# Output-projection weights and the gains of the cross norm: loaded at other places, multiplied in at other places, and one norm handed from VectorE to ScalarE

## The chip, the cores and the metric

One core of one Trainium2 chip runs the whole program. The metric is the device time of one execution in microseconds (us). A core has a matmul engine (TensorE, PE in the rows; its weight loads are listed as PEld), VectorE (DVE), ScalarE (ACT), GpSimd (POOL) and SyncE (SP), which here only issues DMA transfers. Each engine works through its own list of instructions in order and waits on semaphores for the others.

## The reference, cut to what matters

One layer of a decoder on 1024 tokens of width 1024, in fp32: two mixers side by side (a gated short convolution and a sparse attention of 8 heads, 512 columns each), an output projection, cross attention to 256 memory tokens, and a SwiGLU block. The piece around the change is:

```python
def rmsnorm(x, g):
    y = xf * lax.rsqrt(jnp.mean(xf * xf, axis=-1, keepdims=True) + EPS)
    return (y * g.astype(jnp.float32)).astype(x.dtype)

mixed = jnp.concatenate([rmsnorm(y_conv, norm_conv_out), rmsnorm(y_att, norm_attn_out)], axis=-1)
h = h + rmsnorm(mixed @ w_out, norm_mix_post)

hn = rmsnorm(h, norm_x_pre)
mn = rmsnorm(mem, norm_mem)
qx = (hn @ w_q_x).reshape(b, s, X_HEADS, X_HEAD_DIM)
```

The gains `norm_x_pre` scale the columns of `hn`, which are the rows of `w_q_x`: the product is the same whether they are multiplied into the one or into the other.

## The kernel before, in words

Every matrix product is three matmuls: each operand is split into a rounded part `h` and a remainder `l`, and `mm3` (lines 58 to 62) adds h·h, h·l and l·h in PSUM. `split` (lines 64 to 76) makes `h` on ScalarE (line 66) and `l` on VectorE (line 75 or 76). A product of a 128x128 weight tile with 512 columns is one instruction of PE.

The program runs in stages: projections of the input, the attention by tiles of 128 tokens (its last product of values ends at about 661 us of the profile) with other products filled in between, then the stage of the change, the cross attention, and the SwiGLU block. The stage of the change goes as follows. Tiles are named by their stage and token tile: `mixed_t` holds tile t of the mixers' result.

The convolution half of the output projection, `mix_conv` (line 840), is worked during the attention, its products in `pwc`, and lands in `mixed_t`. The attention half needs rows 4 to 7 of `w_out` (`wor_k`, split into `woh_k` and `wol_k` by `wo_weights`, line 863) and the attention's output in transposed form: tiles 0 to 6 come back from DRAM in pairs (`or_0`, `or_2`, `or_4`, `or_6`, line 879), tile 7 straight from PSUM (`pot`, transposed on PE at line 554). `put_o` splits each into `A_h` and `A_l`. `mix_mm` then multiplies tile by tile into `pwa_t` (tiles 0 and 1 together, k outermost), and `mix_evac` (line 1008) adds it to `mixed_t` on VectorE.

`project` (line 955) and `Post` (line 908) carry each tile on: the squares of `mixed_t` are summed on ScalarE (`scr`, line 928), its post norm multiplied and added to the residual `res` (lines 934 and 935, VectorE), `res` spilled to DRAM, its squares summed again, and the next norm, that of the cross attention, written over `mixed_t` (line 942, VectorE, one pass over 128x1024 with the scale of the row and `g_next`, the gains broadcast to all partitions). `turn_in` transposes that on PE (`ptr`, line 950) and splits it into `A_h`, `A_l`. The products with `w_q_x` (`pqx`, `qx_mm`) follow: its column tiles `wq_h_d` are loaded and split by `col_weights` (line 896); the first two are wanted after tile 7 of `pwa`.

The order on each engine is decided by the framework's scheduler from a simulated timeline: instructions are written as above, the scheduler interleaves them, and `issue_after` holds some back behind a named instruction. Tiles with `bufs` rotate through that many buffers, and a load into a buffer waits for the last reader of its old content. Pools on the "right" side take memory from the other end.

## Time and profile before

| | |
|---|---|
| median of 3 runs | 1660.38 us (1659.99 to 1666.0) |
| profiled execution | 1662.39 us |
| its span, from first to last instruction | 1660.7 us |
| mean granted clock of PE | 0.98 |
| busy share of the span: PE, DVE, ACT, POOL | 95 %, 61 %, 46 %, 27 % |

The profile is of one execution. PE is busy 95 % of the span, so the time of the program is that of PE's work, at the clock it is granted, plus PE's waits; a change in what the other engines do shows only where PE waits for them. In a timeline a row gives the start in us from the span's start, the time taken, engine, line and operation (tile written <- tiles read), and in brackets how long the engine idled before it and which instruction released it. Rows of one kind that follow each other are merged (x2 means two).

### The profile page before, as it was taken

The numbers are of one execution on the slowest core, as the hardware profiler recorded it, in microseconds if no ns is written. First come the engines' busy times: TensorE is split into PE (matmuls) and PEld (weight loads), VectorE is DVE, ScalarE is ACT, GpSimd is POOL, SyncE is SP. The second block draws the span as 40 slices with busy tenths as digits, with TensorE's granted clock in tenths as the row PEclk, the third lists the DMA queues.
The fourth block names the chain that finished last, engine by engine and source line by source line (L and its number), as shares of the span: only waits on it lengthen the run. The fifth ranks groups of instructions, "written<-read, shape, count | busy, mean of one in ns | idle before, by whom it ended". The sixth has DMA issues, their size and how long they took to land. (4 is left out here: it accounts for less than half of the span.)

```text
span 1660.7 us, 22653 instructions
## 1 busy us (share of the span) xinstructions
PE 1578.8 (95%) x8095; PEld 1315.2 (79%) x8095; DVE 1008.9 (61%) x1781; ACT 762.0 (46%) x1554; POOL 456.3 (27%) x498
## 2 busy tenths in 40 slices
PE   8898999999999999889998988899999999999997
PEld 6786778887998888678796767688888888788886
DVE  5664456667656683771187597567444444587575
ACT  6433334456776674552285455333323232344453
POOL 0212345344554240000043003565344442000000
PEclk9999999999999999999999999999999999999999
DMA  8234111112620000633342144553333221873351
GB/s 296 66 118 149 39 57 46 51 48 87 203 100 17 20 8 19 228 141 109 109 138 90 52 167 169 163 201 112 110 119 114 103 96 70 321 275 97 100 166 69
DMA packets 78641, 192.59 MB, mean 116 GB/s; under 512 B 9024, under 2 KB 12224, under 8 KB 78528
## 3 DMA queue, kind: packets, MB, share of 16 engines
q1 hardware_dynamic: 73056, 179.08, 31.9%
q10 hardware_dynamic: 4320, 7.87, 1.3%
q0 software_dynamic: 1152, 4.19, 0.7%
q8 instruction: 64, 1.05, 0.3%
q14 instruction: 49, 0.40, 0.1%
HBM read 140.25 MB, written 50.86 MB: 115 GB/s over the span
## 5 line engine op out<-in xcount | busy, mean ns | idle before, releaser
L75 DVE TENSOR_TENSOR tl<-pt,th 128x512 fp32r<-128x512 f32 (+2 forms) x168 | 102.5, 620 | 54.8 <-ACT th L66 52.2
L61 PE MATMUL dp<-dl,ah 128*128 128x512 f32 x308 | 121.2, 394 | 2.2 <-DVE dl L75 2.2
L66 ACT ACTIVATE th<-pt 128x512 fp32r<-128x512 f32 (+2 forms) x168 | 89.2, 544 | 71.3 <-PE pv L653 37.2
L62 PE MATMUL dp<-dh,al 128*128 128x512 f32 x308 | 120.8, 393 | 0.0
L60 PE MATMUL dp<-dh,ah 128*128 128x512 f32 x308 | 118.6, 393 | 0.5 <-ACT dh L66 0.5
L626 POOL TENSOR_SCALAR pw<-pw,rs,gate 128x64 f32<-128x64 f32 (+5 forms) x128 | 76.1, 605 | 115.7 <-DVE rs L624 76.3
L66 ACT ACTIVATE ah<-over_l 128x512 fp32r<-128x512 f32 x77 | 48.5, 630 | 104.0 <-PE dp L61 103.9
L75 DVE TENSOR_TENSOR al<-over_l,ah 128x512 fp32r<-128x512 f32 x77 | 53.2, 690 | 54.3 <-ACT ah L66 53.2
L1103 POOL TENSOR_SCALAR xe<-xe,xsm 128x256 f32<-128x256 f32 x32 | 21.8, 696 | 208.3 <-DVE xsm L1101 202.8
L626 POOL TENSOR_SCALAR ps<-ps,rs,gate 128x128 f32<-128x128 f32 (+7 forms) x64 | 53.6, 840 | 86.1 <-DVE rs L624 43.6
L589 DVE TENSOR_REDUCE nm<-s 128x1 f32<-128x128 f32 (+7 forms) x64 | 47.9, 752 | 38.3 <-PE s L519 38.1
L61 PEld LDWEIGHTS dp<-dl,ah 128*128 128x128 f32 x308 | 58.6, 190 | 14.7 <-DVE dl L75 2.6
L60 PEld LDWEIGHTS dp<-dh,ah 128*128 128x128 f32 x308 | 58.3, 190 | 13.1 <-ACT dh L66 0.9
L62 PEld LDWEIGHTS dp<-dh,al 128*128 128x128 f32 x308 | 58.6, 190 | 12.3
L594 DVE TENSOR_REDUCE nm<-s 128x1 f32<-128x640 f32 (+4 forms) x64 | 41.7, 652 | 41.1 <-PE s L519 40.8
L1456 POOL TENSOR_TENSOR s<-wu 128x512 f32<-128x512 f32 x22 | 30.9, 1405 | 121.4 <-DMA wu<-in_w_gu_dram 20.1
L604 ACT ACTIVATE ps<-s,nm 128x128 f32<-128x128 f32 (+7 forms) x64 | 47.4, 742 | 28.6 <-DVE nm L589 28.6
L609 ACT ACTIVATE pw<-s,nm 128x640 f32<-128x640 f32 (+4 forms) x64 | 42.2, 659 | 31.7 <-DVE nm L595 24.7
L1468 DVE TENSOR_TENSOR u<-pc,u 128x512 f32<-128x512 f32 x22 | 15.2, 691 | 62.9 <-PE pc L62 62.3
L635 PE MATMUL pt<-ident,pw 128*128 128x128 f32 (+1 forms) x304 | 50.2, 273 | 1.6 <-DVE rs L623 1.6
L623 DVE TENSOR_SCALAR rs<-sm 128x1 f32<-128x1 f32 (+1 forms) x128 | 31.2, 246 | 30.4 <-ACT pw L615 20.1
L1482 DVE TENSOR_TENSOR a<-pd,u 128x512 f32<-128x512 f32 x22 | 15.2, 690 | 56.7 <-PE pd L62 56.7
(1495 smaller groups left out, 5275.0 us busy)
## 6 DMA issues: line engine op xcount, KB each, us to landing
over_l<-act_d SPq DMA_DIRECT2D x77, 256.0 KB, 2.7
wg<-in_w_gu_dram SPq DMA_DIRECT2D x22, 512.0 KB, 3.3
wu<-in_w_gu_dram SPq DMA_DIRECT2D x22, 512.0 KB, 3.9
act_d<-a SPq DMA_DIRECT2D x44, 256.0 KB, 2.1
act_d<-as_as SPq DMA_DIRECT2D x33, 256.0 KB, 2.8
h_d<-res SPq DMA_DIRECT2D x16, 512.0 KB, 2.6
res<-h_d SPq DMA_DIRECT2D x16, 512.0 KB, 4.2
over_h<-in_w_down_dram SPq DMA_DIRECT2D x28, 256.0 KB, 5.4
```

Source lines behind the costliest of these rows:

```text
L60: PE.matmul(ps, sh, mh, start=first, stop=False, **kw)
L61: PE.matmul(ps, sh, ml, start=False, stop=False, **kw)
L62: PE.matmul(ps, sl, mh, start=False, stop=last, **kw)
L66: ACT.activation(hi, src, AF.Copy, scale=1.0 if scale is None else scale)
L75: return (DVE if lo_eng == "dve" else POOL).tensor_tensor(lo, src, f32(hi), op=ALU.subtract)
L589: DVE.tensor_reduce(nm[:, r, 0:1], ps[:, :self.ns], axis=AX.X, op=ALU.max, negate=True)
L594: DVE.tensor_reduce(nm[:, r, 1:2], ps[:, self.w0:CM], axis=AX.X, op=ALU.max, negate=True)
L604: ACT.activation(e[:, :self.ns], ps[:, :self.ns], AF.Exp, bias=nm[:, r, 0:1], accum_out=sm[:, r, 0:1])
L609: ACT.activation(e[:, w0:CM], ps[:, w0:CM], AF.Exp, bias=nm[:, r, 1:2], accum_out=sm[:, r, 1:2])
L623: DVE.tensor_scalar(rs[:, r, s0:s1], sm[:, r, s0:s1], 1e-30, None, op0=ALU.max)
L626: POOL.tensor_scalar(e[:, c0:c1], e[:, c0:c1], rs[:, r, x:x + 1], gt[:, gi:gi + 1], op0=ALU.mult, op1=ALU.mult)
L635: PE.transpose(pt[:m, (2 * x + r) * P:(2 * x + r + 1) * P], self.P[b][r][:, c:c + m], ident)
```

## The change

- `g_x`, the gains `norm_x_pre` as 128x8 (partition p, column k holds gain 128k+p), is loaded by a DMA of its own, written in the middle of the program; it waits for nothing, and the scheduler puts it at the program's start, in SP's queue between the loads of `convw` and the fourth of `pr_kv`.
- Loads and splits of `w_out` rows 4 to 7: `wor_4`, `wor_5`, `wor_6` and `or_0` go into a new pool `wr`, issued during the attention; `woh_4` and `wol_4` are split there too. `wor_7` follows the use of `wor_5`'s buffer. The other three splits stay behind the attention.
- The broadcast row `g_next` and its 512 KB load are dropped. The norm of the cross attention in `Post.norm` becomes one ScalarE instruction per tile (8 in all), which multiplies by the row's scale alone.
- `col_weights` multiplies each of the eight `wq` tiles by `g_x` on GpSimd, in place, before its split; its raw tile has 2 buffers everywhere (the later use had 3).

```diff
--- before.py
+++ after.py
@@ -136,6 +136,7 @@
     SP.dma_start(gains, a["gains"])
     g_u, g_mem, g_c = gains[:, 0:NK], gains[:, NK:2 * NK], gains[:, 2 * NK:3 * NK]
 
+    g_x = const.tile([P, NK], F32, name="g_x")
     convw = const.tile([P, NC, 3], F32, name="convw")
 
     ap, close_ap = open_pool("ap")
@@ -848,6 +849,23 @@
 
     for t in range(NT - 5):
         mix_conv(t)
+    wr, close_wr = open_pool("wr", side="right")
+    wh, wl = {}, {}
+    wh[NC], wl[NC] = (wr.tile([P, D], F32R, name=f"wo{c}_{NC}") for c in "hl")
+    wor = {}
+
+    def wo_load(k):
+        wor[k] = wr.tile([P, D], F32, tag="woraw", name=f"wor_{k}", bufs=3)
+        SP.dma_start(wor[k], a["w_out"][k])
+
+    def wo_split(k):
+        split(wh[k], wl[k], wor.pop(k), scale=g_c[:, k:k + 1])
+
+    with nc.allow_non_contiguous_dma("one row of gains as columns"):
+        SP.dma_start(g_x, a["norm_x_pre"].rearrange("(k p) -> p k", p=P))
+    for k in range(NC, NK - 1):
+        wo_load(k)
+    wo_split(NC)
     with tc.issue_after(last_score.ins):
         for t in range(NT - 5, NT):
             mix_conv(t)
@@ -855,15 +873,9 @@
     close_keep()
 
     wo, close_wo = open_pool("wo")
-    wh, wl = {}, {}
-    for k in range(NC, NK):
+    for k in range(NC + 1, NK):
         wh[k] = wo.tile([P, D], F32R, name=f"woh_{k}")
         wl[k] = wo.tile([P, D], F32R, name=f"wol_{k}")
-
-    def wo_weights(k):
-        raw = wo.tile([P, D], F32, tag="woraw", name=f"wor_{k}", bufs=3)
-        SP.dma_start(raw, a["w_out"][k])
-        split(wh[k], wl[k], raw, scale=g_c[:, k:k + 1])
 
     def put_o(t, o):
         at = slice(NC, NK), slice(t * P, (t + 1) * P)
@@ -871,13 +883,16 @@
 
     put_o(NT - 1, tiles_[NT - 1].po)
     for t in range(NT - 1):
-        if t < NC:
-            wo_weights(NC + t)
+        if 0 < t < NC:
+            wo_split(NC + t)
         if t % 2 == 0:
-            raw = wo.tile([P, 2, CONV], F32, tag="woraw", name=f"or_{t}", bufs=3)
+            raw = (wr if t == 0 else wo).tile([P, 2, CONV], F32, tag="woraw" if t == 0 else "or", name=f"or_{t}",
+                                              bufs=3 if t == 0 else 2)
             n = min(2, NT - 1 - t)
             last_o = SP.dma_start(raw[:, :n, :], o_d[t:t + n].rearrange("t p c -> p t c"))
         put_o(t, raw[:, t % 2, :])
+        if t == 1:
+            wo_load(NK - 1)
     close_psum()
     psum, close_psum = open_pool("psum_dense", 1, space=PSUM)
     banks.clear()
@@ -894,10 +909,11 @@
         return hi, lo
 
     def col_weights(pool, name, src, bufs):
-        raw = pool.tile([P, NK, P], F32, tag="craw", name=f"{name}r", bufs=bufs)
+        raw = pool.tile([P, NK, P], F32, tag="craw", name=f"{name}r", bufs=2)
         hi = pool.tile([P, NK, P], F32R, tag="chi", name=f"{name}h", bufs=bufs)
         lo = pool.tile([P, NK, P], F32R, tag="clo", name=f"{name}l", bufs=bufs)
         SP.dma_start(raw, src)
+        POOL.tensor_tensor(raw, raw, g_x.rearrange("p (k o) -> p k o", o=1).to_broadcast([P, NK, P]), op=ALU.mult)
         split(hi, lo, raw)
         return hi, lo
 
@@ -939,7 +955,10 @@
             ss = self.ss
             self.square(self.res, 2)
             rms_scale(ss[:, 3:4], ss[:, 2:3], D)
-            DVE.scalar_tensor_tensor(self.m, self.res, ss[:, 3:4], self.g_next, op0=ALU.mult, op1=ALU.mult)
+            if self.g_next is None:
+                ACT.activation(self.m, self.res, AF.Copy, scale=ss[:, 3:4])
+            else:
+                DVE.scalar_tensor_tensor(self.m, self.res, ss[:, 3:4], self.g_next, op0=ALU.mult, op1=ALU.mult)
 
     def turn_in(s, t, m):
         tk = slice(t * P, (t + 1) * P)
@@ -987,10 +1006,8 @@
 
     wt, close_wt = open_pool("wt")
     g_post = wt.tile([P, D], F32, name="g_post1")
-    g_next = wt.tile([P, D], F32, name="g_next1")
     with tc.issue_after(last_o.ins):
         SP.dma_start(g_post, row_bcast(a["norm_mix_post"]))
-        SP.dma_start(g_next, row_bcast(a["norm_x_pre"]))
     wps = {}
 
     def mix_mm(ts_):
@@ -1026,11 +1043,12 @@
                 qx_weights(wt, 0, 2)
         qx_mm(0, 0, d)
 
-    project(1, mix_mm, mix_evac, lambda t: a["x"][t * P:(t + 1) * P, :], h1_d, wt, g_post, g_next, qx_early)
+    project(1, mix_mm, mix_evac, lambda t: a["x"][t * P:(t + 1) * P, :], h1_d, wt, g_post, None, qx_early)
     for d in range(2):
         qx_mm(0, 1, d)
     close_wt()
     close_wo()
+    close_wr()
     close_mp()
 
 
@@ -1397,7 +1415,7 @@
     def ox_between(n):
         if n == 0:
             for n_, name in enumerate(("norm_x_post", "norm_ffn_pre")):
-                g = og.tile([P, D + (144 if n_ == 0 else 0)], F32, name=f"g_{name}")[:, :D]
+                g = og.tile([P, D + (136 if n_ == 0 else 0)], F32, name=f"g_{name}")[:, :D]
                 SP.dma_start(g, row_bcast(a[name]))
                 gains2.append(g)
         else:
```

The order of the instructions is moved at three places. The first is ScalarE's list at the end of the attention (`osb` is the sum of squares of the attention's tile 7, `pwc_7_*` the last convolution products). Before:

```order
L548 ACTIVATE osb_7_5275,ss_a_88<-otok_7_5658 128x512
L83 ACT_TABLE_LOAD
L83 ACTIVATE r_a_86<-ss_a_88,eps_73 128x8
L847 ACTIVATE mixed_7_7043<-pwc_7_1_7254,r_c_85 128x512
L66 ACTIVATE A_h_96<-pot_7_5661 128x4x128
L66 ACTIVATE woh_4_7273<-wor_4_7283,gains_90 128x1024
L66 ACTIVATE A_h_96<-or_0_7287 128x4x128 x2
L66 ACTIVATE woh_5_7275<-wor_5_7291,gains_90 128x1024
L66 ACTIVATE woh_6_7277<-wor_6_7297,gains_90 128x1024
```

and now:

```order
L848 ACTIVATE mixed_7_7044<-pwc_7_0_7255,r_c_85 128x512
L66 ACTIVATE A_h_97<-or_0_7296 128x4x128 x2
L66 ACTIVATE A_h_97<-or_2_7308 128x4x128 x2
L549 ACTIVATE osb_7_5276,ss_a_88<-otok_7_5659 128x512
L66 ACTIVATE woh_7_7292<-wor_7_7304,gains_90 128x1024
L83 ACT_TABLE_LOAD
L83 ACTIVATE r_a_86<-ss_a_88,eps_73 128x8
L848 ACTIVATE mixed_7_7044<-pwc_7_1_7269,r_c_85 128x512
L66 ACTIVATE A_h_97<-or_4_7316 128x4x128 x2
L66 ACTIVATE A_h_97<-pot_7_5662 128x4x128
L66 ACTIVATE A_h_97<-or_6_7322 128x4x128
L66 ACTIVATE wq_0_0h_7710<-wq_0_0r_7709 128x1024
```

The weights' splits `woh_5` and `woh_6` stand ahead of these rows now; the splits of `or_0` to `or_4` and of `woh_7` have moved ahead of that of `pot_7`. On PE `pwa_0` and `pwa_1` alternated by twos before; now six of `pwa_0` come first, and the first of `pwa_1` waits for VectorE's `A_l` of `pot_7`, whose PSUM bank it takes.

The second is VectorE's list where the first two tiles of the projection leave PSUM. Before:

```order
L75 TENSOR_TENSOR A_l_97<-or_4_7311,A_h_96 128x4x128 x2
L75 TENSOR_TENSOR A_l_97<-or_6_7317,A_h_96 128x4x128
L1008 SCALAR_TENSOR_TENSOR mixed_0_7036<-pwa_0_7332,r_a_86,mixed_0_7036 128x1024
L1008 SCALAR_TENSOR_TENSOR mixed_1_7037<-pwa_1_7333,r_a_86,mixed_1_7037 128x1024
L84 RECIPROCAL ss1_0_7383<-ss1_0_7383 128x1
L934 SCALAR_TENSOR_TENSOR mixed_0_7036<-mixed_0_7036,ss1_0_7383,g_post1_7328 128x1024
```

and now:

```order
L75 TENSOR_TENSOR A_l_98<-pot_7_5662,A_h_97 128x4x128
L75 TENSOR_TENSOR A_l_98<-or_6_7322,A_h_97 128x4x128
L75 TENSOR_TENSOR wq_0_0l_7711<-wq_0_0r_7709,wq_0_0h_7710 128x1024
L1025 SCALAR_TENSOR_TENSOR mixed_0_7037<-pwa_0_7335,r_a_86,mixed_0_7037 128x1024
L1025 SCALAR_TENSOR_TENSOR mixed_1_7038<-pwa_1_7336,r_a_86,mixed_1_7038 128x1024
L75 TENSOR_TENSOR wq_0_1l_7718<-wq_0_1r_7716,wq_0_1h_7717 128x1024
L84 RECIPROCAL ss1_0_7386<-ss1_0_7386 128x1
```

The remainder of the first query weight, `wq_0_0l`, stood behind the evacuation of `pwa_2` and `res1_1`; now it stands ahead of that of `pwa_0`, and that of the second, `wq_0_1l`, behind `pwa_1`. On ScalarE both `wq` splits stand ahead of `scr1_0_0`, and wait for GpSimd's multiplication.

The third is the end of the projection, the last tiles' norms. VectorE before:

```order
L934 SCALAR_TENSOR_TENSOR mixed_7_7043<-mixed_7_7043,ss1_7_7761,g_post1_7328 128x1024
L935 TENSOR_TENSOR res1_7_7762<-res1_7_7762,mixed_7_7043 128x1024
L75 TENSOR_TENSOR A_l_97<-ptr1_5_0_7743,A_h_96 128x4x128
L75 TENSOR_TENSOR A_l_97<-ptr1_5_1_7750,A_h_96 128x4x128
L84 RECIPROCAL ss1_6_7669<-ss1_6_7669 128x1
L942 SCALAR_TENSOR_TENSOR mixed_6_7042<-res1_6_7670,ss1_6_7669,g_next1_7329 128x1024
L84 RECIPROCAL ss1_7_7761<-ss1_7_7761 128x1
L942 SCALAR_TENSOR_TENSOR mixed_7_7043<-res1_7_7762,ss1_7_7761,g_next1_7329 128x1024
```

and ScalarE now:

```order
L944 ACTIVATE scr1_7_0_7769,ss1_7_7766<-mixed_7_7044 128x1024
L959 ACTIVATE mixed_5_7042<-res1_5_7618,ss1_5_7617 128x1024
L83 ACTIVATE ss1_7_7766<-ss1_7_7766,eps_73 128x1
L944 ACTIVATE scr1_6_2_7773,ss1_6_7672<-res1_6_7673 128x1024
L83 ACTIVATE ss1_6_7672<-ss1_6_7672,eps_73 128x1
L959 ACTIVATE mixed_6_7043<-res1_6_7673,ss1_6_7672 128x1024
L66 ACTIVATE A_h_97<-ptr1_5_0_7748 128x4x128
L66 ACTIVATE A_h_97<-ptr1_5_1_7755 128x4x128
```

The norms of line 942 are gone from VectorE's list; ScalarE has them as `mixed_5`, `mixed_6`, each behind the squares it needs (in the changed kernel line 944 is the squares, 959 the norm). The first product of the next weights, `pqx_0_0_1`, still stands behind the transposes of tile 6 on PE.

## Rows read from the trace of the kernel before

**Rows 1.** Waits of PE, 640 to 830 us: line, releaser: total, times, longest.

```profile
PE ptr L950 <- DVE ss L84: 4.2, 1, 4.2
...
PE pwa L60 <- DVE mixed L1008: 2.6, 1, 2.6
PE pwa L60 <- ACT A_h L66: 2.4, 1, 2.4
...
PE pwa L61 <- DVE wol L76: 0.8, 2, 0.5
```

**Rows 2.** Stretches: length; busy PE, PEld, DVE, ACT, POOL; granted clock, DMA, GB/s.

```profile
687.00:690.00 3.00, 3.00 (x9) 2.35 (x8) 2.47 (x5) 1.90 (x6) 0.00 (x0) 0.50 1.02 418
717.00:735.00 18.00, 14.54 (x80) 12.13 (x78) 17.89 (x24) 12.08 (x26) 0.00 (x0) 0.99 0.35 137
736.00:741.00 5.00, 5.00 (x17) 4.23 (x16) 2.33 (x3) 1.19 (x2) 0.00 (x0) 0.50 0.75 270
```

**Rows 3.** Waits of PE from 0 to 50 us, same columns as group 1.

```profile
PE pe L298 <- ACT cmp L286: 3.7, 1, 3.7
```

**Rows 4.** DMA queue from 1.0 to 2.2 us: packets, MB, share of 16 engines.

```profile
q1 hardware_dynamic: 129, 0.01, 8.6%
```

**Rows 5.** DMA queue from 6 to 16 us, same columns.

```profile
q1 hardware_dynamic: 1385, 3.77, 99.4%
```

**Rows 6.** Timeline of ACT near 42 us: start, us, operation [idle before <- releaser].

```profile
41.92 1.06 ACT L199 ACTIVATE xt<-xt 128x1024 f32<-128x1024 f32 x1 [1.27 <-DMA xt<-in_x_dram]
```

**Rows 7.** Timeline of ACT from 655 to 700 us.

```profile
668.63 0.59 ACT L66 ACTIVATE A_h<-pot 128x512 fp32r<-128x512 f32 x1
669.10 1.15 ACT L66 ACTIVATE woh<-wor,gains 128x1024 fp32r<-128x1024 f32 x1
...
693.27 1.06 ACT L66 ACTIVATE wq_0h<-wq_0r 128x1024 fp32r<-128x1024 f32 x1 [1.59 <-DMA wq_0r<-in_w_q_x_dram]
```

**Rows 8.** Timeline of PE from 660 to 692 us.

```profile
667.84 0.60 PE L554 MATMUL pot<-ident,otok 128*128 128x128 f32 x4
...
683.09 0.40 PE L62 MATMUL pwa<-woh,A_l 128*128 128x512 f32 x1
686.08 0.50 PE L60 MATMUL pwa<-woh,A_h 128*128 128x512 f32 x1 [2.60 <-DVE mixed L1008]
...
687.34 0.63 PE L61 MATMUL pwa<-wol,A_h 128*128 128x512 f32 x1
687.77 0.63 PE L62 MATMUL pwa<-woh,A_l 128*128 128x512 f32 x1
```

**Rows 9.** Timeline of SP from 600 to 700 us.

```profile
679.37 0.42 SPq L992 DMA_DIRECT2D g_post<-in_norm_mix_post_dram  x1
```

**Rows 10.** Timeline of POOL near 392 us.

```profile
392.09 2.38 POOL L75 TENSOR_TENSOR fw_13l<-fw_13r,fw_13h 128x1024 fp32r<-128x1024 f32 x1
```

**Rows 11.** Timeline of DVE near 392 us.

```profile
392.16 3.39 DVE L760 SCALAR_TENSOR_TENSOR zc<-z,convw,zc 128x1023 f32<-128x1023 f32 x1 [0.34 <-POOL zc L758]
```

**Rows 12.** Timeline of DVE from 655 to 700 us.

```profile
669.25 0.69 DVE L75 TENSOR_TENSOR A_l<-pot,A_h 128x512 fp32r<-128x512 f32 x1 [0.95 <-ACT A_h L66]
670.28 1.28 DVE L76 SCALAR_TENSOR_TENSOR wol<-wor,gains,woh 128x1024 fp32r<-128x1024 f32 x1 [0.35 <-ACT woh L66]
...
684.75 2.47 DVE L1008 SCALAR_TENSOR_TENSOR mixed<-pwa,r_a,mixed 128x1024 f32<-128x1024 f32 x2
...
695.77 1.22 DVE L75 TENSOR_TENSOR wq_0l<-wq_0r,wq_0h 128x1024 fp32r<-128x1024 f32 x1
```

**Rows 13.** Line 942: count: shortest/median/longest ns, first and last start.

```profile
L942 DVE SCALAR_TENSOR_TENSOR mixed<-res,ss,g_next x8: 1266/1275/1285, 698.1 to 735.7; 128x1024 f32<-128x1024 f32 x8
```

**Rows 14.** Timeline of PE from 715 to 748 us.

```profile
735.70 1.94 PE L950 MATMUL ptr<-ident,mixed 128*128 128x128 f32 x8 [4.16 <-DVE ss L84]
737.29 0.78 PE L60 MATMUL pqx<-A_h,wq_1h 128*128 128x512 f32 x1
```

**Rows 15.** Timeline of ACT from 715 to 756 us.

```profile
747.95 1.06 ACT L66 ACTIVATE wq_0h<-wq_0r 128x1024 fp32r<-128x1024 f32 x1 [0.41 <-ACT qe L1041]
```

## The prediction

> **What bounds the kernel now.** I read the share of busy time first: PE is busy 95 % of its span, so what counts is where PE waits and at what clock it runs. The list of PE's waits around the projection shows what can be had there: 4.2 us for VectorE before the transposes of tile 6, 2.6 us for the evacuation of `pwa_0`, 2.4 us for the split of the attention's output, 0.8 us for weight remainders [rows 1], 10 us together. Behind the two gaps the table of stretches shows a granted clock of 0.50, the 1.2 GHz level, in 687 to 690 and in 736 to 741 us [rows 2]: products there started every 0.43 us [rows 8], and I count nine, against 0.25 in the stretch before (worked out below), so each such gap cost about 9 x 0.18 = 1.6 us more. At the program's start there is one more wait that the change can touch, 3.7 us for `cmp` [rows 3].
>
> **The change part by part.**
>
> *The load of `g_x`.* It is 1024 single values that lie 512 bytes apart in the tile's row order, so no two can share a run. The only small transfer whose packets stand alone is that of the gains, 128 rows of 96 bytes: 129 packets took 8.6 % of 16 engines over 1.2 us [rows 4], 1.65 us of one engine, 13 ns each. 1024 such packets are 13 us of one engine, 0.8 us of all 16. The other bound is the mean packet where `g_x` now goes: 1385 packets filled 99.4 % of the queue for 10 us [rows 5], 115 ns each, which makes 1024 x 115 / 16 = 7.4 us. The queue has no room there, so what `g_x` takes, the later loads come later: the last `xt` already keeps ScalarE waiting 1.27 us [rows 6], and behind its squares come `r_u`, `cmp` and PE's 3.7 us. I pass the delay on in full, and take the near row with a little for the full queue: +1.0 us, bounds 0 and +7.4.
>
> The Trainium skill has a rule that speaks against this load: "DMA: Bandwidth & Descriptors", section "Rules for kernel authors", says that a strided last dimension is lowered to one descriptor per element and should be rearranged. No row of before shows such a transfer. Were it gathered by rows, 128 packets, the term would be 0.1 us.
>
> *`woh_4` and `wol_4` in the attention.* One split is 1.15 us on ScalarE [rows 7] and 1.28 us on VectorE [rows 12]. Both have idle time there, PE has nearly none. I cost it +0.3 us; without cover it is 2.4 us, and the slight reshuffle of the attention may also give back 1 us.
>
> *The end of the attention.* The transposes of `pot` start at 667.84 us and take 0.60 [rows 8]. Before, `pwa_0` then waited 2.4 us. Now weight 4 and `or_0` are there, and six products of `pwa_0` run at once, to about 669.8. The next, the first of `pwa_1`, takes the bank of `pot` and waits for the remainder `A_l` of `pot_7`. In ScalarE's list that split (668.63 before) now has six splits `A_h<-or` of its own size and one `woh` ahead of it, 6 x 0.59 + 1.15 = 4.7 us [rows 7], of which I let 0.6 fit into its idle time (my estimate): it starts at about 672.7, and VectorE's part ends 1.3 us later, as before (669.25 + 0.69 - 668.63) [rows 7, 12], at 674.0. So the wait of 2.4 becomes one of about 4. Before, 48 products took from 670.8 (668.44 and the wait) to 683.5, with 0.8 us of waits in it: 0.247 each [rows 1, 8]. 42 of them from 674.0 end at 684.4, 0.9 us later than before; if this gap lowers the clock as the others did, 1.6 us later still.
>
> *Loads of the query weights.* Before, 13.9 us went by from the issue of `g_post` at 679.37 [rows 9] to the landing of `wq_0r`, which released ScalarE at 693.27 [rows 7]. Now `g_post` follows `or_6`, which waits for VectorE's split of `or_2` at about 668.3; and 512 KB of `g_next` are gone, about an eighth of what was in that queue, 1.3 us. With a less crowded queue I take the landing at 680.5 (679 to 682).
>
> *VectorE at the first evacuation.* `wq_0_0l` now stands ahead of it and waits for GpSimd, then ScalarE. GpSimd's product of two 128x1024 tiles takes 2.38 us [rows 10], ScalarE's part 1.06 [rows 7], the remainder 1.22 and an evacuation 1.24 (two in 2.47) [rows 12]. One more thing: beside that GpSimd product a VectorE instruction with two operands in SBUF took 3.39 us [rows 11], where one of the same form takes 1.28 [rows 13]; it ended about one such length after GpSimd did. The second multiplication (`wq_0_1`) follows the first at once, so `wq_0_0l` will be held until it ends: 680.5 + 2 x 2.38 + 1.22 + 1.24 = 687.7. Without that hold it is 680.5 + 2.38 + 1.06 + 1.22 + 1.24 = 686.4; by the products alone, 684.4 + 1.3 = 685.7, or 687.3 at the low clock. `pwa_2` started at 686.08 before [rows 8]. I take 687.8: +1.7 us (bounds -0.4 and +3.5). What waits behind `wq_0_0l` are both evacuations, so PE itself. The low clock behind this gap stays as it was.
>
> *The norms.* Eight instructions of 1.275 us [rows 13] leave VectorE, 10.2 us, and ScalarE gets eight of about 1.06 (its pass over a 128x1024 tile, as for `wq_0h` [rows 7]). In the middle of the projection PE does not wait for them. At the end it does: VectorE is busy 17.9 of the 18 us from 717 to 735 [rows 2], and its norm of tile 6 lets the transposes start at 735.70 after 4.16 us of waiting; they take 1.94 at the low clock, so that `pqx` goes on at 737.29 [rows 14]. Two norms stood on VectorE ahead of that of tile 6 in its last ten microseconds, and its own: without them tile 6's residual is done about 2.5 us earlier, and its norm, on ScalarE behind the squares, at about 731.2. PE is then still at the transposes of tile 5, which end at 731.5; those of tile 6 take about half of 1.94 at full clock, and `pqx` goes on at 732.5 to 733.0 instead of 737.29. With the gap goes the low clock behind it. That is -4.5 - 1.6 = -6.1 us (bounds -4.2 and -6.6). Next late would be tile 7's transposes: its norm by the same count at 736.3, before the 24 products of `pqx` end at 738.
>
> *The later query weights.* Six more multiplications, 2.38 each, and one raw buffer less. Their splits did not wait for loads before: the first, at 747.95, was released by ScalarE's own work [rows 15]. I take 0; if the chain of two buffers is late once, +2.4.
>
> Sum: 1.0 + 0.3 + 1.7 - 6.1 = -3.1 us, 1659.3 us for an execution like the profiled one (1662.39, of which 1660.7 are its span). That one lies 2.0 us over the median, so beside the runs shown the forecast is 1660.38 - 3.1 = 1657.3 us.
>
> **The rivals.**
>
> *The preload pays in full.* If the split of `pot_7` is early and the query weights land before the evacuations want them, the 48 products run from 668.45, end at 680.3, and `pwa_2` starts at 681.7, 4.4 us before its old time; a gap that short may leave the clock up, 1.6 more. With the norms, the start and the attention: -6.0 - 6.1 + 1.3 = -10.8, 1649.6 us. For it: the loads are early. Against it: the order of ScalarE's list.
>
> *Slower: the query weight holds VectorE.* Each us by which `wq_0_0r` lands after 680.5 moves the evacuation of `pwa_0`, and PE with it, by one. If SP's queue is not earlier than before and it lands at 693.3, that is +12.8 on the forecast, 1670.1 us. It turns the change into a loss once the landing is later than 680.5 + 3.1 = 683.6. For it: seven loads of 512 KB still share the queue there. Against it: SP's loads hang on instructions that come ten us earlier.
>
> *Slower: one packet per value at the price of the full queue.* 7.4 us in place of 1.0 makes 1663.7 us, 3.3 over before. For it: the queue is full, and the packets stand ahead of loads that PE wants. Against it: the mean packet carries 2.7 KB, `g_x`'s four bytes. The Trainium skill's rule named above is the one by which the packets are that many.
>
> *The norms do not help.* If ScalarE, which now has squares, splits and norms in one list, is as late with tile 6 as VectorE was, the term of -6.1 is gone: 1663.4 us. For it: the norm of tile 5 and that of tile 6 both stand behind squares there. Against it: ScalarE was idle for several us on either side of that place.
>
> **How the numbers follow.** Chances: forecast 0.55 (its own range 1653 to 1661), full preload 0.10, query weight late 0.13, packets dear 0.12, norms no help 0.10. A measurement of this kernel can tell about 0.5 % from no change, 8.3 us: under 1652.1 is faster, over 1668.7 slower. Under it lie the full preload and a rest of the forecast, 0.13; over it half of the late query weight and some mishap with the attention's order, 0.08; the rest, 0.79, is within. The range of 1650 to 1666 leaves out most of the full preload and of the late query weight, and takes in the other cases.
>
> **What would show it.** The transposes of tile 6 without a wait, and `pqx` behind them at full clock, show the norms' term; a wait for `ptr` or a granted clock of 0.50 there shows it wrong. The first product of `pwa_1` with about 4 us of waiting for VectorE's `A_l`, and `pwa_2` waiting for `mixed` until about 687.8, show the two junctions; `wq_0_0l` longer than 1.22 us shows the hold. The wait of `pe` for `cmp`, 3.7 before, shows the price of `g_x`. The forecast is wrong if PE's waits in 640 to 750 us do not shrink by some 3 us together, or if the time moves in stages that the change does not touch.

## The result: 0.6 % slower, and where the time went

The changed kernel takes 1673.02 us (median of 8 runs, 1667.55 to 1674.97) against 1662.87 of the kernel before on the same chip (8 runs, 1659.99 to 1666.0). The ratio is 1.0057, 95 % interval 1.0038 to 1.0075. The forecast was 1657.3 us, 3.1 less than the 1660.38 known then, and the range ended at 1666. The forecast is wrong in sign. The profiled execution took 1669.5 us with a span of 1667.8, 7.1 more than before, at the same mean clock (0.981 and 0.98). Line numbers have moved: 298 is now 299, 942 is 959 (on ScalarE) or 961, 950 is 969, 1008 is 1025; 865 loads `g_x`, 916 multiplies by it.

### The stage of the change: near the forecast, and faster

The waits of PE in the profile after, 640 to 760 us (line, releaser: total, times, longest):

```profile
PE pwa L60 <- DVE A_l L75: 3.6, 1, 3.6
PE pqx L60 <- DVE A_l L75: 1.0, 1, 1.0
PE pwa L60 <- DVE mixed L1025: 0.7, 1, 0.7
...
PE ptr L969 <- DVE A_l L75: 0.5, 1, 0.5
```

The 4.2 us before the transposes of tile 6 are gone, and the 2.6 for `pwa_0`'s evacuation are 0.7; in place of the 2.4 for `A_h` [rows 1] stand 3.6 for the `A_l` of `pot_7`. PE's timeline after (start, us, operation, idle before) shows the three places:

```profile
672.34 0.60 PE L555 MATMUL pot<-ident,otok 128*128 128x128 f32 x4
672.69 0.48 PE L60 MATMUL pwa<-woh,A_h 128*128 128x512 f32 x1
...
677.91 0.80 PE L60 MATMUL pwa<-woh,A_h 128*128 128x512 f32 x1 [3.58 <-DVE A_l L75]
678.51 0.63 PE L61 MATMUL pwa<-wol,A_h 128*128 128x512 f32 x1
...
691.24 0.50 PE L60 MATMUL pwa<-woh,A_h 128*128 128x512 f32 x1 [0.72 <-DVE mixed L1025]
...
736.42 0.66 PE L969 MATMUL ptr<-ident,mixed 128*128 128x128 f32 x4 [0.54 <-DVE A_l L75]
737.02 0.51 PE L60 MATMUL pqx<-A_h,wq_1h 128*128 128x512 f32 x1
```

The transposes of `pot` start 4.5 us later than before (667.84 [rows 8]), since what lies ahead took longer. Six products of `pwa_0` run at once, then comes the gap of 3.6 us, and behind it products start every 0.43 us instead of 0.23. At the end `pqx` follows the transposes without the old gap. The table of stretches of the same profile (columns as in [rows 2]):

```profile
679.00:683.00 4.00, 4.00 (x11) 3.13 (x10) 0.00 (x0) 0.00 (x0) 0.00 (x0) 0.50 1.03 420
717.00:735.00 18.00, 18.00 (x95) 15.04 (x94) 15.02 (x21) 15.01 (x28) 0.00 (x0) 1.00 0.35 133
736.00:741.00 5.00, 4.58 (x21) 3.69 (x22) 2.32 (x5) 3.47 (x7) 0.88 (x1) 1.00 0.84 277
```

The clock of 0.50 now lies behind the new gap, and no longer behind 736 us; from 717 to 735 PE has no idle time. The eight norms on ScalarE:

```profile
L959 ACT ACTIVATE mixed<-res,ss x8: 1138/1151/1159, 701.0 to 738.5; 128x1024 f32<-128x1024 f32 x8
```

They take 1.15 us each where the sum had 1.06, and end in time. The query weights, in the timelines of SP, POOL, ACT and DVE after:

```profile
675.91 0.53 SPq L915 DMA_DIRECT2D wq_0r<-in_w_q_x_dram  x1
```

```profile
685.15 1.90 POOL L916 TENSOR_TENSOR wq_0r<-wq_0r,g_x 128x1024 f32<-128x1024 f32 x1 [39.04 <-DMA wq_0r<-in_w_q_x_dram]
687.01 1.90 POOL L916 TENSOR_TENSOR wq_1r<-wq_1r,g_x 128x1024 f32<-128x1024 f32 x1
```

```profile
676.36 0.58 ACT L66 ACTIVATE A_h<-pot 128x512 fp32r<-128x512 f32 x1
...
687.08 1.06 ACT L66 ACTIVATE wq_0h<-wq_0r 128x1024 fp32r<-128x1024 f32 x1 [9.63 <-POOL wq_0r L916]
```

```profile
677.18 0.68 DVE L75 TENSOR_TENSOR A_l<-pot,A_h 128x512 fp32r<-128x512 f32 x1
...
688.17 1.81 DVE L75 TENSOR_TENSOR wq_0l<-wq_0r,wq_0h 128x1024 fp32r<-128x1024 f32 x1 [9.72 <-ACT wq_0h L66]
689.91 2.46 DVE L1025 SCALAR_TENSOR_TENSOR mixed<-pwa,r_a,mixed 128x1024 f32<-128x1024 f32 x2
```

`wq_0_0l` stands ahead of the evacuation, as the order showed, and takes 1.81 us instead of 1.22 [rows 12] beside the second multiplication. From the start of `pot`'s transposes to that of the last row of transposes of `mixed_7` PE took 77.0 us before and 70.4 now. Six more kernels further down have the instructions of before in this stage, and took 73.2 to 76.7 us there: the profile of before is the longest of the seven.

### The stage that no edit is in: slower

The table of stretches shows where the time went. From 1100 to 1400 us both kernels work the gate and up products of the SwiGLU block, from 1500 to 1640 its down products. Before, in the columns of [rows 2]:

```profile
1100.00:1400.00 300.00, 300.00 (x1312) 246.26 (x1311) 158.15 (x214) 93.14 (x145) 133.90 (x101) 1.00 0.33 111
1500.00:1640.00 140.00, 140.00 (x619) 115.98 (x618) 94.76 (x146) 65.96 (x117) 0.00 (x0) 1.00 0.35 106
```

and after:

```profile
1100.00:1400.00 300.00, 300.00 (x1287) 241.35 (x1286) 153.51 (x210) 91.55 (x142) 130.17 (x98) 1.00 0.32 109
1500.00:1640.00 140.00, 140.00 (x620) 115.91 (x619) 99.00 (x153) 67.77 (x121) 0.00 (x0) 1.00 0.36 110
```

PE never idles in either, the granted clock is 1.00 in both, and yet 1312 products have become 1287: one every 0.2331 us instead of every 0.2287. The down products are as fast as before (620 and 619). The whole gate and up stage took 381.98 us before and 389.39 now: 7.4 us, more than the 7.1 between the two spans, and three quarters of the 10.2 between the medians. The other stages of the two profiles nearly cancel: +1.3 us up to the first `pcv`, +3.2 in the attention, -6.6 in the projection, +1.3 in the query stage, +0.4 in the cross attention, +0.1 behind the gate and up products. In PE's own rows the products after, one behind the other, read

```profile
1199.67 0.40 PE L61 MATMUL pd<-xR_l,s_9h 128*128 128x512 f32 x1
1199.90 0.39 PE L62 MATMUL pd<-xR_h,s_9l 128*128 128x512 f32 x1
1200.14 0.39 PE L60 MATMUL pd<-xR_h,s_9h 128*128 128x512 f32 x1
1200.37 0.40 PE L61 MATMUL pd<-xR_l,s_9h 128*128 128x512 f32 x1
```

No row shows a wait: the pitch itself has changed.

What differs for these products is where their operands lie in SBUF. `g_x` is a tile of 32 bytes in each partition in the pool `const`, which is laid out first, so every later tile of the left side moves up by 32 bytes; the tiles of the right side stay. The gate and up products have the moving operand (`x_*`, `xR_*`) on the left and the stationary one (the split weights, `s_*` and the like) on the right; the down products have both on the right. By the sizes of the tiles the moving operands start at 288 bytes, modulo 1024, before and at 320 after, the stationary ones at 992: their distance was 704 and is 672. This is the distance of the tiles' starts. The blocks of a weight tile lie 512 bytes apart (128 values), so the products of every second block have 512 less, 192 before and 160 now. The down products' operands both start at 864: distance 0. The diff itself answers to the shift at one place: the padding in `ox_between` goes from 144 to 136 values, 32 bytes less, which keeps the tiles behind it where they were.

### The profile page after: what moved, and what is told of

It reads as the page before. It is cut to its first block, busy times and chain, and to the rows that moved or that the text cites. A ratio compares the mean times of both kernels' runs of the same rounds, so it can differ in the third digit from the quotient of the medians.

```text
span 1667.8 us, 22673 instructions
## 1 busy us (share of the span) xinstructions
PE 1588.2 (95%) x8095; PEld 1313.0 (79%) x8095; DVE 998.4 (60%) x1773; ACT 770.4 (46%) x1562; POOL 471.0 (28%) x506
## 3 DMA queue, kind: packets, MB, share of 16 engines
q8 instruction: 64, 1.05, 0.3%
## 5 line engine op out<-in xcount | busy, mean ns | idle before, releaser
L1486 DVE TENSOR_TENSOR u<-pc,u 128x512 f32<-128x512 f32 x22 | 15.2, 692 | 64.8 <-PE pc L62 64.2
L636 PE MATMUL pt<-ident,ps 128*128 128x128 f32 x288 | 48.5, 283 | 1.3 <-DVE tl L75 1.3
```

The costliest lines, as they stand in the source:

```text
L636: PE.transpose(pt[:m, (2 * x + r) * P:(2 * x + r + 1) * P], self.P[b][r][:, c:c + m], ident)
```

## The experiments

All kernels ran in five rounds beside the kernel before. "Distance" is that of the stationary from the moving operand of the gate and up products, modulo 1024 bytes. The stages are worked out from the starts of rows in PE's timelines, as the profile merges them: attention from the first `pcv` to the last `pot`, projection from there to the last `ptr` of the stage, query stage on to the first `psx`, gate and up from the first `pd` to the first `dp`; each from one profile. The ratio is to the kernel before, with its 95 % interval.

| kernel | distance | attention | projection | query | gate, up | ratio |
|---|---|---|---|---|---|---|
| before | 704 | 505.3 | 77.0 | 82.55 | 381.98 | |
| after | 672 | 508.5 | 70.4 | 83.82 | 389.39 | 1.0057 (1.0038 to 1.0075) |
| e1: before, left +32 | 672 | 514.1 | 76.0 | 83.82 | 389.39 | 1.0095 (1.0069 to 1.0120) |
| e2: before, left +64 | 640 | 508.6 | 74.2 | 83.86 | 387.79 | 1.0069 (1.0043 to 1.0096) |
| e3: before, left +32, right -32 | 640 | 510.1 | 73.2 | 83.85 | 387.79 | 1.0085 (1.0063 to 1.0106) |
| e4: after, left +32 more | 640 | 511.2 | 70.0 | 83.54 | 387.80 | 1.0069 (1.0047 to 1.0091) |
| e5: before, both -32 | 704 | 506.3 | 73.8 | 82.55 | 381.98 | 1.0004 (0.9988 to 1.0021) |
| e14: before, left -32 | 736 | 509.2 | 76.7 | 83.83 | 389.38 | 1.0071 (1.0044 to 1.0098) |
| e11: before, left -320 | 0 | 506.3 | 74.2 | 81.90 | 378.31 | 0.9971 (0.9953 to 0.9989) |
| e6: after, left at its old place | 704 | 505.6 | 71.9 | 82.55 | 381.98 | 1.0007 (0.9986 to 1.0028) |
| e9: norms and query weights alone | 704 | 506.4 | 70.9 | 82.58 | 382.00 | 0.9971 (0.9949 to 0.9993) |
| e10: output weights alone | 704 | 505.4 | 74.2 | 82.55 | 382.00 | 0.9991 (0.9970 to 1.0011) |
| e13: after's parts, reordered | 704 | 510.9 | 69.3 | 82.58 | 381.98 | 1.0003 (0.9984 to 1.0022) |
| e15: e13 better ordered, left -320 | 0 | 509.3 | 64.2 | 81.92 | 378.29 | 0.9922 (0.9894 to 0.9950) |

### Is it the address, and which one? e1 to e4

e1 and e2 are the kernel before, with 32 or 64 unused bytes behind `convw` and the padding cut by as much; e3 moves the left side by 32 and lays 32 unused bytes under the right side, too (with one memset of them on GpSimd); e4 is the changed kernel with `g_x` in 64 bytes.

```diff
-    convw = const.tile([P, NC, 3], F32, name="convw")
+    convw = const.tile([P, NC * 3 + 8], F32, name="convw")[:, :NC * 3].rearrange("p (c j) -> p c j", j=3)   # e1, e3; +16 in e2
...
+    rp, close_rp = open_pool("rp", side="right")                  # e3
+    rpad = rp.tile([P, 8], F32, name="rpad")
...
-    g_x = const.tile([P, NK], F32, name="g_x")                    # e4, from after
+    g_x = const.tile([P, 2 * NK], F32, name="g_x")[:, :NK]
```

> The kernel before, with nothing changed but 32 unused bytes per partition behind convw: every tile allocated from the left after it lies 32 bytes further, those from the right stay; the instructions and their order are those of before. Theory A (the products whose stationary and moving operands no longer lie at the same offset modulo 64 bytes run slower: conv products 300 to 380 us and the gate/up products 1053 to 1435 us, at 0.2333 us against 0.2285 per product): 7 to 7.5 us longer in 1053 to 1435 us, 1.5 us in 100 to 380, in all +8 to +10 us, about 1671. Rival B (the slower products of the changed kernel come from its instructions, or from the chip that ran it): no difference, 1660 to 1666.

> As e1, with 64 unused bytes instead of 32. Theory A (offset modulo 64): no difference from before, 1660 to 1666, and the gate/up products at 0.2285 us. Rival C (any move away from the old addresses, or less free memory, costs it): about +9, 1671.

> The kernel before with 32 bytes on the left and 32 on the right, so that both operands of all products move from offset 32 to offset 0 modulo 64. Theory A1 (it is the difference of the two operands' offsets that costs): no difference from before, 1660 to 1666. Theory A2 (it is the offset of the moving operand by itself): +9 or more, 1671 and above, and the down products (dp), whose operands both lie on the right, slower too.

> The changed kernel with the tile of g_x 64 bytes wide instead of 32 (only half is used): instructions and order as in the changed kernel, left tiles at offset 32 modulo 64 again. Theory A: the gate/up products at 0.2285 us again, 8 to 9 us less than the changed kernel, 1663 to 1665, so about -0.5 to +2 us against before; the forecast's own sum (-3.1) would be 1659.8 beside a median of 1662.9. Rival B (its instructions or the chip): 1673 as before the edit.

e1 has every instruction of before in its old order, and 32 unused bytes. It is slower by 0.95 % (0.69 to 1.20), 16 us (11 to 20), which more than covers the change's loss. Its gate and up products, and those of e3:

```profile
1100.00:1400.00 300.00, 300.00 (x1287) 241.34 (x1286) 154.71 (x210) 91.69 (x142) 132.10 (x100) 1.00 0.33 111
```

```profile
1100.00:1400.00 300.00, 300.00 (x1293) 243.19 (x1292) 157.32 (x213) 91.30 (x142) 132.53 (x100) 1.00 0.32 111
```

e1 counts 1287 products as the changed kernel does. That 64 bytes would restore the old speed, since only the address modulo 64 mattered, fell with e2 and e4. e3 has e1's left addresses and yet e2's 387.79 us, to the hundredth: the left address alone does not decide, the distance does.

### Equal distance at other addresses, and the parts at the old ones: e5, e6, e9, e10

e5 and e6 put two small tiles into one, which moves the left side down by 32 bytes; e5, from before, adds e3's right-side pool, e6, from after, the padding of 144. e9 has the norm on ScalarE and the multiplied query weights, with `g_x` as a fourth group in the load of `gains`, and nothing of the output weights; e10 has the output weights' part of the diff alone.

```diff
-    r_m = const.tile([P, 2], F32, name="r_m")                     # e5, e6, e9
-    ss_m = const.tile([P, 2], F32, name="ss_m")
+    rs_m = const.tile([P, 4], F32, name="rs_m")
+    r_m, ss_m = rs_m[:, 0:2], rs_m[:, 2:4]
...
-    gains = const.tile([P, 3 * NK], F32, name="gains")            # e9
+    gains = const.tile([P, 4 * NK], F32, name="gains")
+    g_x = gains[:, 3 * NK:4 * NK]
```

> The kernel before with two small tiles laid into one, which moves all later left tiles 32 bytes down, and 32 bytes taken at the top of the right side, which moves all right tiles 32 bytes down: the distance from every left tile to every right one is that of before, all absolute addresses differ. So far the gate/up stage (first pd to first dp) took 381.98 us before, 389.39 at a distance changed by 32 bytes (changed kernel, e1) and 387.79 at one changed by 64 (e2, e3, e4). Theory A1 (the distance between the two operands decides): 382.0 us there and no difference from before in all. Rival C (the old addresses by themselves are good): 387 to 390 and +8 to +12 in all.

> The changed kernel with the same two small tiles laid into one, so that g_x takes no new room: every tile that both kernels have and that the change does not move on purpose lies where it lay before, instructions and order as in the changed kernel. Theory A (the addresses are what the forecast missed): gate/up 382.0 us, 9 to 10 us less than the changed kernel in all, and so 0 to 4 us less than before (the forecast's sum was -3.1). Rival D (the changed kernel is slower for other reasons too, its clock in the attention or the junction): +3 or more against before.

> The kernel before with the norm part alone: g_x as eight more columns of the gains tile (no load of single values), multiplied into wq by GpSimd, the norm by ScalarE, g_next dropped; W_out's loads as before; addresses as before. Forecast's own terms: the tail's -6.1 and a junction of 0 to +1.7: -4 to -6 us against before, the 4.2 us of waiting before the transposes of tile 6 gone. Rival (the norms do not help, or the query weight in front of the evacuation eats it): -1 to +3.

> The kernel before with the W_out part alone (loads of rows 4 to 6 and of or_0, and the first split, during the attention), addresses of the other tiles as before. By the forecast: the 2.4 us wait of pwa_0 becomes one of 3.5 to 4 of pwa_1 for the split of pot_7, the low clock behind it costs 1.6: 0 to +2 us against before. Rival (the preload pays): -3 to -6, no wait above 1 us ahead of pwa.

e5 moved both sides, and nothing changed: 381.98 us, ratio 1.0004. Distance again, not address. e6 is the whole change without the shift: the gate and up stage is back at 381.98 and 1312 products, and the total at that of before (-2.3 to +4.7 us).

```profile
1100.00:1400.00 300.00, 300.00 (x1312) 246.15 (x1311) 158.99 (x214) 92.32 (x143) 132.90 (x101) 1.00 0.32 112
```

The waits from 640 to 760 us of e9, and then of e10:

```profile
PE pwa L60 <- ACT A_h L66: 2.4, 1, 2.4
PE pwa L60 <- DVE mixed L1011: 1.9, 1, 1.9
PE ptr L955 <- ACT mixed L945: 1.0, 2, 0.5
```

```profile
PE ptr L962 <- DVE ss L84: 4.2, 1, 4.2
PE pwa L60 <- DVE A_l L75: 3.5, 1, 3.5
```

The parts are separate: the norms cut the wait for `ptr` from 4.2 us to two of 0.5, and gain 0.29 % (0.07 to 0.51), 4.8 us; the output weights trade a wait of 2.4 for one of 3.5, and their total is unchanged within the interval.

### Another distance, and a better order: e11, e13, e14, e15

e14 is e5 without the right-side pool. e11 is the kernel before with `identb` and `ones` in a later pool of the left side (`keep`) and the merge of e5, so that `A_h` and the gate and up operands come 320 bytes lower. e13 holds the late splits behind `pot_7` and the `wq` multiplication behind the second evacuation, with `g_x` in `gains` as in e9, at the old distance; e15 writes `pot_7`'s split out so that ScalarE's part comes first, and adds distance 0 (for which `r_u` moves to `keep`, too).

```diff
-    identb = const.tile([P, P], BF, name="identb")                # e11, e15
+    identb = keep.tile([P, P], BF, name="identb")
...
-        put_o(t, raw[:, t % 2, :])                                # e13; hi7 in e15
+        with tc.issue_after(low7.ins) if t > 1 else ExitStack():
+            if t == NC - 1:
+                wo_split(NC + t)
+            put_o(t, raw[:, t % 2, :])
...
+        with tc.issue_after(behind) if behind is not None else ExitStack():   # behind = the evacuation of pwa_1
```

> The kernel before with the two small tiles laid into one: left tiles 32 bytes lower, right ones in place, a distance of 736 modulo 1024. By distance the gate/up stage took 381.98 us at 704, 389.39 at 672 and 387.79 at 640. Theory A1: not the value of before again, since the distance differs: 387 to 390, +8 to +12. Rival (only less distance costs, or only a move upwards): 382, no difference.

> The kernel before with two small const tiles laid into one and two others (identb, ones) allocated in the attention's pool, so that the tiles from A_h on and the gate/up operands lie 320 bytes lower: left operands (offset 288 modulo 1024 before) now at 992, like the right ones; instructions and order unchanged. The down products, whose operands lie at equal offsets modulo 1024 in every kernel, start every 0.2267 us on average, the gate/up products every 0.2285 before and 0.2325 to 0.2335 at the other distances. Theory E (equal offsets are the best distance): gate/up about 379 us instead of 381.98, conv products shorter too, -3 to -5 us in all. Rival F (the old distance of 704 was a lucky one, this one is like the rest): 387 to 390 and +8 to +12.

> The changed kernel at the old addresses, with g_x as columns of the gains tile, the splits of or_2 to or_6 and of woh_7 held behind that of pot_7, and GpSimd's multiplication and the splits of the first two query weights held behind the evacuation of tile 1. By the forecast's own steps the 3.5 us wait of pwa_1 and the low clock behind it go, and VectorE evacuates pwa_0 at once: the stretch from the last pot to the last ptr, 71.9 us with the changed kernel at old addresses (e6), 77.0 before, comes to 64 to 67; -7 to -10 us against before. Rival (another wait takes the place of these, the query weights come late for pqx): 70 and more there, -2 to 0.

> All parts together: the changed kernel with g_x as columns of the gains tile, ScalarE's split of pot_7 now held ahead of those of or_2 to or_6 and of woh_7 (in e13 only VectorE's part was held, and pwa_1 still waited 3.3 us), the query weights behind the evacuation of tile 1, and identb, ones and r_u allocated in the attention's pool, so that left and right operands lie at equal offsets modulo 1024 as in e11. By the terms measured so far: gate/up 378.3 us (-3.7), conv and query products about -1, the stretch from the last pot to the last ptr 64 to 67 us against 74 to 77 with the kernel before (e13 had 69.3 with the wait of 3.3): -9 to -13 us against before, ratio 0.992 to 0.995. Rival (the gains do not add, something next is late): -3 to -6 as e9 or e11 alone.

e14 is slower by 0.71 % though it saves 32 bytes: at 32 bytes either way from 704 the stage is as slow. The gate and up products of e14, and of e11, at distance 0:

```profile
1100.00:1400.00 300.00, 300.00 (x1288) 240.98 (x1287) 154.49 (x211) 90.34 (x140) 131.88 (x99) 1.00 0.33 111
```

```profile
1100.00:1400.00 300.00, 300.00 (x1325) 248.43 (x1324) 161.09 (x216) 92.88 (x144) 133.73 (x101) 1.00 0.34 114
```

e11 has 1325 products in the same 300 us, 0.2264 us each, which is the pitch of the down products (140 us through 619: 0.2262), whose distance is 0 in every kernel. e11 is 0.29 % (0.11 to 0.47) faster than before with none of its work changed.

e13 failed in its aim: only VectorE's part of `pot_7`'s split was held in front, and the wait stayed. The waits of e13, and of e15, from 640 to 760 us:

```profile
PE pwa L60 <- DVE A_l L75: 3.3, 1, 3.3
PE pwa L60 <- DVE mixed L1027: 1.5, 1, 1.5
PE ptr L971 <- ACT mixed L961: 1.3, 1, 1.3
```

```profile
PE pqx L60 <- DVE A_l L75: 1.0, 1, 1.0
...
PE pwa L60 <- DVE A_l L885: 0.5, 1, 0.5
```

e15 has both gaps closed, 64.2 us in the projection against 77.0, and the short pitch. It takes 1650.24 us, 0.78 % (0.50 to 1.06) less than before, 13 us: the fastest kernel here.

## Why the prediction was wrong

**The step that failed** is the sum, 1.0 + 0.3 + 1.7 - 6.1: it has a term for what each edit issues and none for where its tile lies. `g_x` was costed as a DMA alone; that its 32 bytes move every left-side operand against the right side was not weighed, though the diff shows the tile at the head of `const` and a padding that answers to it. The prediction named time that moves in stages the change does not touch only as a condition for being wrong. That condition came true: the term left out is +7.4 us in the gate and up stage and +1.3 in the query stage, 8.7 together, and e6, the change without the shift, is 0.5 % or 8 us better than the change. That is two thirds of the 12.6 us between the forecast of -3.1 and the +9.5 of the ratio; the rest, some 4 us, is what e6 misses, and is located below in one profile only.

The attention is longer, too, in the six kernels at 640, 672 and 736 (508.5 to 514.1 us, against 505.3 to 506.4 in the five at 704 in the order of before or of the change). But there it is the clock. The stretch from 395 to 450 us, before, after, in e1 and in e13:

```profile
395.00:450.00 55.00, 51.72 (x389) 47.28 (x390) 44.28 (x89) 41.81 (x86) 31.88 (x27) 0.97 0.58 191
395.00:450.00 55.00, 52.18 (x372) 47.24 (x371) 42.19 (x79) 38.54 (x82) 28.70 (x24) 0.91 0.54 178
395.00:450.00 55.00, 52.17 (x347) 47.27 (x346) 40.79 (x79) 38.55 (x79) 27.43 (x23) 0.84 0.54 178
395.00:450.00 55.00, 52.33 (x349) 47.46 (x348) 40.94 (x80) 38.91 (x80) 28.48 (x25) 0.84 0.53 178
```

By the clock records of the traces the attention had a granted clock of 0.50, half of the full one, for 5.5 us before, 11.4 after and 23.1 in e1. Half of what was added, 3.0 and 8.8 us, is what the stage is longer, 3.2 and 8.8. With half of that time taken off, the attention is 502.5 to 504.2 us in the six and 502.6 to 503.8 in the five. Whether the shift brings the low clock is open: e13 has it, too, at the old distance but in another order, with 510.9 us. By itself the shift costs 16 us (11 to 20) by e1, and 11 to 14 by e2, e3 and e14; 8.7 of e1's 16 are the two stages' pitch, and the rest is not located beyond its one profile.

**The norms, -6.1.** The mechanism was right: transposes without the wait, `pqx` at full clock, as written. The size is less sure. From the start of `pwa_2` to that `pqx` PE took 51.2 us before (686.08 to 737.29 [rows 8, 14]) and 45.8 after, -5.4 where the sum had -4.5. e9's total is 4.8 us shorter (1.2 to 8.5). That its projection is 6.1 shorter, the forecast to the tenth, is luck: against the other six profiles with the instructions of before, 73.2 to 76.7 us, it is 2.3 to 5.8.

**The end of the attention, +1.7 in all.** The mechanism was right and its sizes nearly so: a gap of 3.6 us for `pot_7`'s `A_l` where I said about 4, and the low clock behind it. Counted from the start of `pot`'s transposes, since all of it lies 4.5 us later, the query weight landed after 12.8 us (forecast 12.7), and `pwa_2` started after 18.9 (forecast 20.0). `wq_0_0l` was held as said: it ended at 689.98, 1.07 us after the second multiplication. But GpSimd's multiplications take 1.90 us instead of the 2.38 taken from a subtraction of two whole tiles (line 75, which the prediction calls a product). Taken together, the projection became 6.6 us shorter than in the profile of before, and 2.8 to 6.3 shorter than in the other six, where the sum had 1.7 - 6.1 = -4.4.

**The load of `g_x`, +1.0.** Its price in the queue is the near row's; its price in PE's time is not resolved. In the DMA part of the profile after (whole run, then the load from 0 to 40 us), and in ACT's timeline:

```profile
DMA packets 79537, 192.07 MB, mean 115 GB/s; under 512 B 10048, under 2 KB 13248, under 8 KB 79424
...
g_x<-in_norm_x_pre_dram SPq DMA_DIRECT2D x1, 4.0 KB, 6.8
```

```profile
42.97 1.06 ACT L200 ACTIVATE xt<-xt 128x1024 f32<-128x1024 f32 x1 [1.26 <-DMA xt<-in_x_dram]
```

Packets under 512 bytes were 9024 before: 1024 more, one for each value. This agrees with the rule of the Trainium skill, "DMA: Bandwidth & Descriptors", section "Rules for kernel authors", that a strided last dimension becomes one descriptor per element. The queue from 8 to 16 us, where they go, before and after:

```profile
DMA packets 1156, 3.08 MB, mean 385 GB/s; under 512 B 381, under 2 KB 411, under 8 KB 1156
DMA packets 2125, 2.91 MB, mean 363 GB/s; under 512 B 1417, under 2 KB 1417, under 8 KB 2125
```

It moved 0.17 MB less, which at the 385 GB/s of before is 0.4 us of the full queue. In the trace a packet of four bytes takes 9 ns there, 1024 of them 0.6 us of 16 engines: neither the 115 ns nor the 7.4 us of the far bound. The last `xt` starts 1.05 us later than before [rows 6], and PE's wait for `cmp` is 4.4 us where it was 3.7 [rows 3]; but that wait is 1.2 in e6 with the load and 4.0 in e15 without, and the start to the first `pe` spreads from 43.7 to 46.9 us over the profiles with or without it.

**The whole change at the old addresses.** e6 gives +1.2 us (-2.3 to +4.7) where the sum had -3.1, a little below the interval. Its projection is 5.1 us shorter, and in the two profiles the cross attention, from the first `psx` to the first `pd`, takes it back: 225.9 us before, 230.9 in e6.

```profile
827.39:1053.31 225.92, 199.74 (x982) 164.75 (x983) 168.46 (x239) 132.22 (x281) 54.28 (x54) 0.94 0.39 131
820.98:1051.89 230.91, 203.09 (x983) 167.63 (x983) 168.79 (x239) 132.84 (x281) 54.01 (x54) 0.92 0.37 128
```

The granted clock is 0.94 in the one and 0.92 in the other; it was at 0.50 for 26.7 and for 37.5 us, and half of the difference, 5.4, covers the 5.0. What lowers it is open: with the instructions of before the stage took 221.3 us in e1, at 0.97, and 230.4 in e2, at 0.92. One more difference is a wait: before the transposes of the norm behind the cross attention (`ptr<-ident,y`, near 979 us) PE waits 3.8 to 3.9 us for VectorE in each of the five kernels with both parts (after, e4, e6, e13, e15), 1.1 to 1.3 in before, e1, e2, e9 and e14, and 2.6 to 2.7 in e3, e5, e10 and e11. Its price was not measured alone.

**The rivals.** None was it. The query weight landed on its forecast place; the packets were as many as feared, at 9 ns each and not at 115; the norms helped; and the full preload, which the change missed by the order of ScalarE's list, is what e15 has.

## What to carry to other kernels

A tile added to the pool that is laid out first moves every operand behind it, so work out what it does to the distance of the stationary from the moving operand, or put it where nothing follows. When a stage that no edit touches gets longer at full clock and without waits, count its products in a window of fixed length: a changed pitch shows there at once. And judge an edit with the addresses held: the same norms that gain 0.3 % look like part of a loss when 32 bytes come with them. A stage of one profile is not enough for a few us, either: with the same instructions the projection spread over 3.8 us between profiles, and the cross attention over 9.

## What the runs showed of the hardware

The pitch of products of 128x128 by 128x512 (operands fp32r) depends on the distance of their two operands' addresses in SBUF. The same stage takes 378.3 us at 0, 382.0 at 704, 387.8 at 640 and 389.4 at 672 and 736, modulo 1024 bytes, each equal within 0.03 us over all kernels with that distance (two at 0, six at 704, three at 640, two at 672, one at 736), at a granted clock of 1.00. Five distances were tried, and 704 stands between two slow neighbours 32 bytes away. Since half of the products lie at 512 bytes less than the distance given, these kernels cannot tell a period of 1024 from one of 512; what in the chip makes it was not tested.

The Trainium skill, "SBUF — State Buffer", section "Who interferes with whom", gives TensorE two independent read ports, one for the moving operand and one for the weight load, and says that TensorE never waits on anyone. The measurement does not contradict that for other engines, but the two operands of TensorE itself are not without effect on each other: 25 products of 1312 were lost to 32 bytes.
